# Applying the RMSNorm row factor after the up projection in a two-layer decoder trunk

## The chip, the cores and the metric

The kernel runs on one core of one Trainium2 chip. The metric is the device time of one execution in microseconds. A core has a matrix engine (TensorE, PE in the rows, with its weight loads as PEld), VectorE (DVE), ScalarE (ACT), GpSimd (POOL) and SyncE (SP), and 16 DMA engines. Matmul results land in PSUM banks, all other tiles lie in SBUF.

## What is computed

One inference step of a two-layer decoder trunk for a prompt of 1024 tokens and 8 single-token samples that share the weights. Layer 0 mixes with an RG-LRU, layer 1 with windowed attention; both add attention over a memory. The change lies in the second part of each layer: the output projection, the norm ahead of the feed-forward network, and its up projection, a depthwise convolution of width 3 over tokens, and the gating.

```python
def _rmsnorm(x, g):
    r = lax.rsqrt(jnp.mean(x32 * x32, axis=-1, keepdims=True) + EPS)
    return (x32 * r * g.astype(jnp.float32)).astype(x.dtype)
...
def _conv_ffn(x, buf, w_up, cw, cb, w_down):
    u = x @ w_up
    u, nbuf = _causal_dwconv(u, buf, cw, cb)
    return (jax.nn.gelu(u[..., :D_FF]) * u[..., D_FF:]) @ w_down, nbuf
...
        x = x + jnp.concatenate([main, mo], axis=-1) @ prm['w_out'][l]
        hn = _rmsnorm(x, prm['norm_ffn_g'][l])
        f, fc = _conv_ffn(hn, ffn_conv0[l], prm['w_ffn_up'][l], ...)
        x = x + f
```

The model width is 1024, the network's inner width 3072 (so the up product has 6144 columns), all in float32. The row factor `r` is one number for each token.

## The kernel before

**Layout.** Activations are kept transposed: 128 features on the partitions, 1032 tokens (1024 prompt, 8 sample) along the free axis, so a tensor of 1024 features is eight row tiles (`KD`). Tokens are cut into two halves of 516 (`HALF`) and four quarters of 258 (`QW`). Each float32 product is made of three matmuls in a reduced format: both operands are split into a high part (a ScalarE copy, L105) and a low part (raw minus high, on POOL, L116, or DVE, L113), and `mm3` (L296) issues high×high (L298), high×low (L299), low×high (L300).

**Output projection** (`out_proj`, L775). For each token half and each of eight feature tiles `m`, 24 matmuls for either quarter go to a PSUM bank, and DVE adds the bank to the residual row `x[m]` (L786). `residual` (L769) loads that row when tile `m` begins in the first half, from the input in layer 0 and from a spilled copy in layer 1. `on_tile` (L1322) then stores the quarter to DRAM (`rD`, from SP's queue), squares it on ScalarE and adds it into a running sum. The weight of the next tile is loaded and split one tile ahead: `get` issues a 1024-column copy on ScalarE and a subtraction on POOL.

**Norm and operands.** The up projection is a 2×2 block product in seven products P1 to P7 instead of eight, on blocks B11, B21, B22 and their combinations T1 to T4 (of the row tiles 0–3 and 4–7 and of the two quarters of a half). When a half of `out_proj` is done, `norm(hf)` (L1345) starts: `inverse` (L1332) sums over features by a matmul with ones (L1335) and forms `r` by Ln, Exp and a correction step; then DVE scales each row by gain and `r`, forms the T blocks and splits all seven sets of four operands. It is a generator that is advanced once a tile. So half 0's norm runs beside half 1's tiles and half 1's beside the first products of the up projection; `need` forces what a product still lacks.

**Up projection** (`ffn`, L862). The columns are taken as 24 pairs `j` of a gate tile and a value tile. `ENTRY` gives pair 0's fourteen half-products, then `SEQUENCE` the seven products of each pair over both halves, 24 matmuls a product. `combine` makes each product's weight: sums and differences of four raw blocks on POOL (four 512-column ops for a pair), a copy on ScalarE, a subtraction on POOL, so eleven POOL ops and seven copies a pair, five products ahead (`AHEAD`). The results are added up from PSUM into the gate row `ug` and the value row `uv` by DVE (two evictions of 258 columns for a product, ScalarE for P1 and P2). After P3 the task `post(j)` convolves both rows (one ScalarE pass each, two DVE taps each, and an add of 128x8 for the sample columns), takes the gelu on ScalarE, multiplies on DVE and stores the gated row to `gD` from SP's queue (L888). Each task goes on by one step a product (`tick`). The down projection reads `gD` and `rD` back.

**Order.** ScalarE keeps the written program order in layer 0 up to L1536 and in the second layer's `ffn` (manual schedule, L62). All other engines, and ScalarE elsewhere, get their order from a scheduler that models time. SP issues every transfer of the program before the change.

## Time and profile before

| | us |
|---|---|
| median of three runs | 2533.31 |
| lowest, highest | 2531.02, 2534.02 |
| the profiled execution | 2532.97 |
| its span | 2531.2 |
| layer 0: output projection and pair 0 (335.3 to 521.7) | 186.4 |
| layer 0: up projection of pairs 1 to 23 (521.7 to 990.2) | 468.5 |
| layer 1: output projection and pair 0 (1614.9 to 1783.9) | 169.0 |
| layer 1: up projection of pairs 1 to 23 (1783.9 to 2252.8) | 468.9 |

The page gives each engine's busy time over the whole span. "Windows" cut the span into stretches and give busy time, instructions and the granted TensorE clock (1.00 is the 2.4 GHz level, 0.50 the 1.2 GHz one; a value between is a mixture). "Waits" sum up an engine's idle time by what ended it. "Timeline" lists single instructions or runs of like ones, with the idle time before them and its releaser. "Groups by form" add up all instructions of one line and shape. Matmuls of the two projections have 258 columns.

### The profile page before, as it was taken

The numbers are of one execution on the slowest core, as the hardware profiler recorded it, in microseconds if no ns is written. First come the engines' busy times: TensorE is split into PE (matmuls) and PEld (weight loads), VectorE is DVE, ScalarE is ACT, GpSimd is POOL, SyncE is SP. The second block draws the span as 40 slices with busy tenths as digits, with TensorE's granted clock in tenths as the row PEclk, the third lists the DMA queues.
The fourth block names the chain that finished last, engine by engine and source line by source line (L and its number), as shares of the span: only waits on it lengthen the run. The fifth ranks groups of instructions, "written<-read, shape, count | busy, mean of one in ns | idle before, by whom it ended". The sixth has DMA issues, their size and how long they took to land. (4 is left out here: it accounts for less than half of the span.)

```text
span 2531.2 us, 42857 instructions
## 1 busy us (share of the span) xinstructions
PE 2336.5 (92%) x16590; PEld 2251.5 (89%) x16590; DVE 1549.6 (61%) x2826; ACT 1103.5 (44%) x2277; POOL 1428.0 (56%) x1123
## 2 busy tenths in 40 slices
PE   7997877799999999999989988787999999999999
PEld 5896866799999999999977787677999999999999
DVE  6658955666666666332478789875666566663321
ACT  5567753344433444211365577643443444442110
POOL 2149843588888885322144346435888888853220
PEclk9998989899999999999999999899999999999999
DMA  4221124212222225421575543551222222253311
GB/s 163 87 69 56 58 83 143 63 67 84 84 85 76 76 76 199 150 95 52 178 252 162 185 152 129 163 157 63 77 86 82 76 76 76 76 224 123 101 55 63
DMA packets 142491, 273.64 MB, mean 108 GB/s; under 512 B 28544, under 2 KB 85456, under 8 KB 142288
## 3 DMA queue, kind: packets, MB, share of 16 engines
q1 hardware_dynamic: 142288, 270.91, 31.9%
q8 instruction: 130, 2.13, 0.3%
q14 instruction: 73, 0.60, 0.1%
HBM read 211.99 MB, written 58.87 MB: 107 GB/s over the span
## 5 line engine op out<-in xcount | busy, mean ns | idle before, releaser
L116 POOL TENSOR_TENSOR row<-row,row 128x512 fp32r<-128x512 f32 (+9 forms) x754 | 1153.8, 1552 | 793.9 <-ACT row L105 476.4
L298 PE MATMUL ps<-row,row 128*128 128x258 f32 (+4 forms) x5032 | 1510.4, 303 | 55.5 <-ACT row L105 45.7
L299 PE MATMUL ps<-row,row 128*128 128x258 f32 (+4 forms) x5032 | 1509.1, 302 | 22.5 <-DVE row L113 18.7
L300 PE MATMUL ps<-row,row 128*128 128x258 f32 (+4 forms) x5032 | 1472.7, 301 | 23.5 <-POOL row L116 23.5
L298 PEld LDWEIGHTS ps<-row,row 128*128 128x128 f32 x5032 | 962.3, 191 | 73.9 <-ACT row L105 51.0
L299 PEld LDWEIGHTS ps<-row,row 128*128 128x128 f32 x5032 | 964.0, 192 | 40.2 <-DVE row L113 24.3
L300 PEld LDWEIGHTS ps<-row,row 128*128 128x128 f32 x5032 | 948.4, 192 | 34.1 <-POOL row L116 27.1
L105 ACT ACTIVATE row<-row 128x512 fp32r<-128x512 f32 (+8 forms) x768 | 505.4, 696 | 911.7 <-POOL row L116 305.4
L113 DVE TENSOR_TENSOR row<-row,ps 128x258 f32<-128x258 f32 (+2 forms) x736 | 322.3, 444 | 706.0 <-PE ps L300 666.5
L119 DVE SCALAR_TENSOR_TENSOR row<-row,fw,row 128x1023 f32<-128x1023 f32 x192 | 266.9, 1409 | 67.3 <-ACT row L105 67.3
L113 DVE TENSOR_TENSOR row<-row,row 128x258 fp32r<-128x258 f32 (+8 forms) x262 | 232.9, 912 | 31.3 <-ACT row L105 18.0
L105 ACT ACTIVATE row<-ps 128x258 f32<-128x258 f32 (+6 forms) x430 | 157.5, 406 | 69.6 <-PE ps L300 25.8
L116 POOL TENSOR_TENSOR row<-row,ty 128x768 f32<-128x768 f32 (+2 forms) x56 | 77.2, 1378 | 155.1 <-DVE ty L413 51.3
L105 ACT ACTIVATE row<-row,fw 128x1032 f32<-128x1032 f32 x96 | 114.9, 1245 | 68.8 <-DVE row L113 68.7
L105 ACT ACTIVATE sm<-row 128x258 f32<-128x258 f32 (+3 forms) x130 | 54.5, 452 | 153.5 <-DVE row L113 127.2
L113 DVE TENSOR_TENSOR row<-row,sb 128x8 f32<-128x8 f32 x96 | 102.3, 1066 | 0.0
L113 DVE TENSOR_TENSOR sm<-sm,sm 128x258 f32<-128x258 f32 (+5 forms) x125 | 81.9, 660 | 28.2 <-ACT sm L105 25.7
L105 ACT ACTIVATE row<-ps,ty,ty 128x256 f32<-128x256 f32 (+1 forms) x160 | 87.4, 564 | 10.1 <-DVE ty L113 7.6
L105 ACT ACTIVATE sm<-ps 128x384 f32<-128x384 f32 (+5 forms) x156 | 65.0, 444 | 39.2 <-PE ps L431 21.6
L113 DVE TENSOR_TENSOR row<-ps,row 128x384 fp32r<-128x384 f32 (+2 forms) x125 | 63.5, 519 | 25.1 <-ACT row L105 10.2
L119 DVE SCALAR_TENSOR_TENSOR row<-sm,pack,row 128x384 f32<-128x384 f32 (+1 forms) x54 | 62.6, 1162 | 14.6 <-POOL row L124 13.3
L116 POOL TENSOR_TENSOR sm<-sm,row 128x192 f32<-128x192 f32 (+3 forms) x72 | 49.5, 702 | 36.1 <-ACT sm L105 18.6
(163 smaller groups left out, 1497.3 us busy)
## 6 DMA issues: line engine op xcount, KB each, us to landing
row<-in_w_ffn_up SPq DMA_DIRECT2D x96, 512.0 KB, 3.3
gD<-row SPq DMA_DIRECT2D x48, 516.0 KB, 2.6
row<-gD SPq DMA_DIRECT2D x48, 516.0 KB, 5.6
row<-in_w_ffn_down SPq DMA_DIRECT2D x64, 384.0 KB, 3.1
row<-hD SPq DMA_DIRECT2D x48, 512.0 KB, 6.6
row<-in_w_out SPq DMA_DIRECT2D x32, 512.0 KB, 4.2
rD<-row SPq DMA_DIRECT2D x64, 129.0 KB, 1.9
row<-rD SPq DMA_DIRECT2D x16, 516.0 KB, 8.7
```

What stands on the lines that cost most here:

```text
L105: return nc.scalar.activation(out, in_, func, **kw)
L113: return V.tensor_tensor(out=out, in0=a, in1=b, op=op)
L116: return G.tensor_tensor(out=out, in0=a, in1=b, op=op)
L119: return V.scalar_tensor_tensor(out=out, in0=a, scalar=s, in1=b, op0=op0, op1=op1)
L298: T.matmul(out, ah, bh, start=first and j == 0, stop=False, skip_group_check=more)
L299: T.matmul(out, ah, bl, start=False, stop=False, skip_group_check=more)
L300: T.matmul(out, al, bh, start=False, stop=last and j == n - 1, skip_group_check=more)
```

## The change

The row factor leaves the operands. The gain is applied when a tile of the output projection is finished: DVE adds PSUM and residual into a small tile, ScalarE writes it back scaled by the gain, stores the small tile to `rD` from its own queue and squares it. The blocks T2, T3, T4 are formed and split during `out_proj` from these unscaled rows (`combine_x`, one row pair as soon as its two tiles are there, hence the tile order `TILES`), and B11, B21, B22 and T1 by 516-column splits afterwards (`settle`). `norm` is gone. The inverse root of all four quarters is formed at the eighth half-product (`factor`) into one row, and DVE multiplies that row into each pair's finished `uv` after P4 and into `ug` after P3 (`scale`).

Residual rows are fetched one ahead, by half. `combine` works in place in the raw weight rows (`PREPARED` gives the order), with eleven POOL ops a pair as before, and pair 0's weights are made during the first half of `out_proj` instead of the second. In `post` the value row is convolved first, gelu comes two steps later, and the gated row is stored from ScalarE's queue. The sample columns are taken out of these steps: `samples` finishes them for twelve pairs at once on POOL. The transposes of layer-0 sample memory attention come two steps later, and two output stores move behind `out_proj`.

```diff
+PREPARED = ("P1", "P7", "P6", "P2", "P5", "P4", "P3")
...
+TILES = (0, 4, 1, 5, 2, 6, 3, 7)
...
         yield
+        yield
+        yield
         t = ps()
         for k in range(2):
...
-    def residual(l, m):
+    def residual(l, hb, kk):
+        t = row()
         if l:
-            return unspill(m)
-        t = row()
-        SY.dma_start(t[:, :NT], I["x_t"][:, m, :])
+            unspill(t, hb, kk)
+        else:
+            SY.dma_start(
+                t[:, : 2 * HALF].rearrange("p (a t) -> p a t", a=2),
+                I["x_t"].rearrange("p (a k) t -> p a k t", a=2)[:, :, kk, hb * HALF : hb * HALF + HALF],
+            )
         return t
...
     def out_proj(l, mget, ks, x, on_tile, on_half):
+        ahead = deque((hb, kk) for hb in range(2) for kk in range(4))
+
+        def fetch():
+            if ahead:
+                hb, kk = ahead.popleft()
+                x[hb, kk] = residual(l, hb, kk)
+
+        fetch()
         for hb in range(2):
-            for m in range(KD):
+            for m in TILES:
                 key = f"out{l}.{hb}.{m}"
                 wh, wl = get(key, 1, 1)
-                if x[m] is None:
-                    x[m] = residual(l, m)
-                for q in (2 * hb, 2 * hb + 1):
-                    c0 = QB[q]
+                if m < 4:
+                    fetch()
+                for part in range(2):
+                    c0 = QB[2 * hb + part]
                     p = ps()
                     mm3(p[:, :QW], [(wh[:, k * P : k * P + P], wl[:, k * P : k * P + P]) + mget(k, c0, QW) for k in ks])
-                    vtt(x[m][:, c0 : c0 + QW], x[m][:, c0 : c0 + QW], p[:, :QW], add)
-                    on_tile(q, m)
+                    on_tile(hb, part, m, p[:, :QW])
                     tick()
                 drop(key)
...
-                src = R["G"][:, lo_]
+                src = G[:, lo_]
+            elif name == "P7":
+                src = G[:, lo_]
+                gtt(src, src, V_[:, lo_], sub)
             elif name == "P6":
-                S = R["S"] = row()
-                gtt(S[:, lo_], R["V"][:, lo_], R["V"][:, hi_], add)
-                gtt(S[:, hi_], S[:, lo_], R["G"][:, lo_], sub)
-                src = S[:, hi_]
+                src = G[:, lo_]
+                gtt(src, V_[:, hi_], src, sub)
             elif name == "P2":
-                src = R["G"][:, hi_]
-            elif name == "P7":
-                src = R["G"][:, lo_]
-                gtt(src, src, R["V"][:, lo_], sub)
+                src = G[:, hi_]
             elif name == "P5":
-                src = R["S"][:, lo_]
+                src = V_[:, lo_]
+                gtt(src, src, V_[:, hi_], add)
             elif name == "P4":
-                src = R["V"][:, hi_]
+                src = V_[:, hi_]
             else:
-                src = R["S"][:, hi_]
-                gtt(src, R["G"][:, hi_], src, sub)
+                src = G[:, hi_]
+                gtt(src, src, G[:, lo_], sub)
             w = row(F32R)
             acopy(w[:, lo_], src)
             gtt(w[:, hi_], src, f(w[:, lo_]), sub)
...
+        def scale(u):
+            vtt(u[:, :NT], u[:, :NT], factor()[:, :NT], mul)
...
-            vtt(a[:, SEQ:NT], a[:, SEQ:NT], sb3[:, :, t], add)
...
         def post(j):
             ug, uv = st.pop(j)
+            scale(ug)
+            av = act_conv(uv, KF + j)
+            yield
+            taps(av, uv, KF + j)
+            del uv
             ag = act_conv(ug, j)
             yield
             taps(ag, ug, j)
             del ug
-            av = act_conv(uv, KF + j)
-            yield
-            taps(av, uv, KF + j)
-            del uv
-            act(ag[:, :NT], ag[:, :NT], AF.Gelu_apprx_tanh)
-            yield
-            vtt(ag[:, :NT], ag[:, :NT], av[:, :NT], mul)
-            SY.dma_start(gD[l, j], ag[:, :NT])
-            yield
+            yield
+            act(ag[:, :SEQ], ag[:, :SEQ], AF.Gelu_apprx_tanh)
+            yield
+            vtt(ag[:, :SEQ], ag[:, :SEQ], av[:, :SEQ], mul)
+            if j % SG == SG - 1:
+                samples(j - SG + 1)
+            yield
+            nc.scalar.dma_start(gD[l, j, :, :SEQ], ag[:, :SEQ])
+
...
+            if name == "P4" and hfs[-1] == 1:
+                scale(st[j][1])
             if name == "P3" and hfs[-1] == 1:
                 return start(post(j))
...
-        todo = [(0, p) for p in STEADY] + [(j, p) for j, p, _ in SEQUENCE if j]
+        todo = [(j, p) for j in range(KF) for p in PREPARED]
         at = 7
         for q, (j, name, hfs) in enumerate(SEQUENCE):
-            if q == 6:
+            if q == 2:
                 load_pair(1)
-            want = 7 if q < 10 else min(len(todo), q - 7 + AHEAD)
+            if q == 8:
+                factor()
+            want = 7 + max(0, q - 4) // 2 if q < 14 else min(len(todo), q - 7 + AHEAD)
...
-        def on_tile(q, m):
-            SY.dma_start(rD[l, m, :, cols(q)], x[m][:, cols(q)])
...
+        def on_tile(hf, part, m, p):
+            q = 2 * hf + part
+            xs, t = place(hf, part, m), sm()
+            vtt(t[:, :QW], xs, p, add)
+            acopy(xs, t[:, :QW], scale=g_ffn[l][m])
+            nc.scalar.dma_start(rD[l, m, :, QB[q] : QB[q] + QW], t[:, :QW])
...
+                s = sm()
+                act(s[:, :QW], t[:, :QW], AF.Square)
+                vtt(sums[q][:, :QW], sums[q][:, :QW], s[:, :QW], add)
+            if part == 0 and wait:
+                combine_x(*wait.pop())
+            if part == 1 and m >= 4:
+                wait.append((hf, m - 4))
+
+        def combine_x(hf, kk):
+            a, b = place(hf, 0, kk), place(hf, 1, kk)
+            c, d = place(hf, 0, kk + 4), place(hf, 1, kk + 4)
+            t3, t2, t4 = (sm()[:, :QW] for _ in range(3))
+            vtt(t3, d, b, sub)
+            vtt(b, b, a, sub)
+            vtt(t2, d, b, sub)
+            vtt(t4, c, t2, sub)
+            for name, t in (("T3", t3), ("T2", t2), ("T4", t4)):
+                if kk % 2 == 0:
+                    own[name] = row(F32R)
+                o = (kk % 2) * HALF
+                split(name, kk, hf, own[name][:, o : o + QW], own[name][:, o + QW : o + HALF], t)
...
+        def settle(hf):
+            cs = slice(hf * HALF, hf * HALF + HALF)
+            for kk in range(4):
+                for a, names in enumerate((("B11", "T1"), ("B21", "B22"))):
+                    k = kk + 4 * a
+                    hi, lo, raw = mh[k][:, cs], ml[k][:, cs], x[hf, kk][:, a * HALF : a * HALF + HALF]
+                    acopy(hi, raw)
+                    (gtt if a else vtt)(lo, raw, f(hi), sub)
+                    for part, name in enumerate(names):
+                        o = slice(hf * HALF + part * QW, hf * HALF + part * QW + QW)
+                        ops[name, kk, hf] = mh[k][:, o], ml[k][:, o]
+                del x[hf, kk]
+                yield
...
         def inverse(q):
+            if not rf:
+                rf.append(row())
             a = sums.pop(q)
             p = ps()
...
+            m, t, r = sm()[:, :QW], sm()[:, :QW], a[:, :QW]
             ts(V, m, p[:, :QW], 1.0 / D, EPS, mul, add)
-            act(out, m, AF.Ln)
...
-        def norm(hf):
-            qa, qb = cols(2 * hf), cols(2 * hf + 1)
-            ra, rb = inverse(2 * hf), inverse(2 * hf + 1)
...
+            act(r, m, AF.Ln)
+            act(r, r, AF.Exp, scale=-0.5)
+            stt(t, m, -0.5, r, mul, mul)
+            vtt(t, t, r, mul)
+            stt(rf[0][:, QB[q] : QB[q] + QW], t, 1.5, r, add, mul)
...
-            for name in STEADY:
+            for name in PREPARED:
                 weights[1](0, name)
                 yield
...
+        gen["w"] = spawn(first_pair())
...
         def on_half(hf):
+            if wait:
+                combine_x(*wait.pop())
             if hf:
                 finish(gen["w"])
-            gen[hf] = start(norm(hf))
-            if not hf:
-                gen["w"] = spawn(first_pair())
+            gen[hf] = start(settle(hf))
...
+        def factor():
+            for q in sorted(sums):
+                inverse(q)
+            return rf[0]
```

ScalarE in the second half of layer 0's output projection, a tile and the next weight's split (the last row), before: `sm` rows are squares, 1024 columns a weight, the 258-column copies `norm`'s operands.

```order
L105 ACTIVATE sm_4219<-row_3601 128x258
L105 ACTIVATE row_3484<-row_3805 128x258
L105 ACTIVATE row_4229<-row_3805 128x258
L105 ACTIVATE row_3488<-row_3873 128x258
L105 ACTIVATE row_4229<-row_3873 128x258
L105 ACTIVATE sm_4268<-row_3601 128x258
L105 ACTIVATE row_3460<-row_3941 128x258
L105 ACTIVATE row_4278<-row_3941 128x258
L105 ACTIVATE row_3464<-row_4009 128x258
L105 ACTIVATE row_4278<-row_4009 128x258
L105 ACTIVATE row_4290<-row_4141 128x512
L105 ACTIVATE row_4293<-row_4190 128x1024
```

And after: `sm`, `pack` to `row` is the scaled row written back, `rD` a store, three copies from `sm` the T blocks.

```order
L108 ACTIVATE row_4339<-row_4269 128x1024
L108 ACTIVATE row_4193<-sm_4372,pack 128x258
L1374 DMA rD<-sm_4372 128x258
L108 ACTIVATE sm_4376<-sm_4372 128x258
L108 ACTIVATE row_4386<-sm_4379 128x258
L108 ACTIVATE row_4389<-sm_4380 128x258
L108 ACTIVATE row_4392<-sm_4381 128x258
L108 ACTIVATE row_4193<-sm_4420,pack 128x258
L1374 DMA rD<-sm_4420 128x258
L108 ACTIVATE sm_4424<-sm_4420 128x258
L108 ACTIVATE row_4427<-row_4343 128x1024
```

The operand copies of `norm` are gone; between two weight splits stand two write-backs, two stores, two squares and, in this tile, three operand copies.

DVE in one pair of the up projection, before: 258-column rows are evictions from `ps`, the taps are on line L119, `row_7419` and `row_7425` are the two convolved rows.

```order
L119 SCALAR_TENSOR_TENSOR row_7419<-row_7258,fw,row_7419 128x1023
L113 TENSOR_TENSOR row_7419<-row_7419,sb 128x8
L119 SCALAR_TENSOR_TENSOR row_7425<-row_7222,fw,row_7425 128x1023
L113 TENSOR_TENSOR row_7425<-row_7425,sb 128x8
L119 SCALAR_TENSOR_TENSOR row_7419<-row_7258,fw,row_7419 128x1022
L119 SCALAR_TENSOR_TENSOR row_7425<-row_7222,fw,row_7425 128x1022
L113 TENSOR_TENSOR row_7493<-row_7457,ps_7467 128x258
L113 TENSOR_TENSOR row_7493<-row_7457,ps_7480 128x258
L113 TENSOR_TENSOR row_7419<-row_7419,row_7425 128x1032
```

And after: `row_4954` is the row of factors, `row_7468` the value row, `row_7502` the gate row; the taps are on line L122.

```order
L116 TENSOR_TENSOR row_7468<-row_7468,row_4954 128x1032
L116 TENSOR_TENSOR row_7502<-row_7502,ps_7575 128x258
L116 TENSOR_TENSOR row_7502<-row_7502,ps_7588 128x258
L116 TENSOR_TENSOR row_7502<-row_7502,row_4954 128x1032
L122 SCALAR_TENSOR_TENSOR row_7664<-row_7468,fw,row_7664 128x1023
L122 SCALAR_TENSOR_TENSOR row_7664<-row_7468,fw,row_7664 128x1022
L122 SCALAR_TENSOR_TENSOR row_7669<-row_7502,fw,row_7669 128x1023
L116 TENSOR_TENSOR row_7736<-row_7702,ps_7710 128x258
L116 TENSOR_TENSOR row_7736<-row_7702,ps_7723 128x258
L122 SCALAR_TENSOR_TENSOR row_7669<-row_7502,fw,row_7669 128x1022
L116 TENSOR_TENSOR row_7669<-row_7669,row_7664 128x1024
```

Two products of 1032 columns have come in and the two 8-column adds have gone. The second product and three taps stand ahead of the next pair's evictions.

## Rows read from the trace of the kernel before

**Rows 1.** Page, part 1: busy time, share of the span, instructions of each engine.

```profile
PE 2336.5 (92%) x16590; PEld 2251.5 (89%) x16590; DVE 1549.6 (61%) x2826; ACT 1103.5 (44%) x2277; POOL 1428.0 (56%) x1123
```

**Rows 2.** Windows, layer 0: stretch, us, busy time (instructions) by engine, clock, DMA share, GB/s.

```profile
335.30:352.00 16.70, 7.98 (x28) 6.50 (x29) 11.99 (x21) 5.75 (x13) 5.91 (x4) 0.50 0.16 41
335.30:405.50 70.20, 53.82 (x384) 51.07 (x384) 29.40 (x53) 21.70 (x45) 28.43 (x17) 0.86 0.41 125
405.50:413.10 7.60, 1.81 (x8) 1.32 (x6) 1.80 (x5) 2.05 (x3) 1.70 (x1) 0.80 0.57 181
413.10:485.00 71.90, 55.30 (x387) 53.79 (x386) 48.72 (x82) 26.79 (x61) 43.31 (x32) 0.83 0.27 86
485.00:521.70 36.70, 27.39 (x172) 23.80 (x171) 29.00 (x65) 14.76 (x40) 15.79 (x19) 0.86 0.19 62
```

**Rows 3.** Windows, layer 1: the same columns.

```profile
1614.90:1674.10 59.20, 54.61 (x424) 52.69 (x421) 40.54 (x86) 26.57 (x55) 25.54 (x15) 0.97 0.88 258
1674.10:1680.90 6.80, 2.54 (x7) 1.43 (x7) 4.08 (x11) 2.09 (x5) 0.06 (x1) 0.67 0.27 97
1680.90:1746.60 65.70, 51.58 (x387) 50.62 (x385) 41.37 (x81) 25.72 (x57) 40.52 (x30) 0.88 0.19 63
1746.60:1783.90 37.30, 27.90 (x173) 24.29 (x172) 28.93 (x65) 14.83 (x40) 15.82 (x19) 0.86 0.18 61
```

**Rows 4.** Waits of TensorE, 335.3 to 521.7: waited for, total us, times, longest.

```profile
PE ps L298 <- ACT row L105: 26.7, 10, 8.2
PE ps L300 <- POOL row L116: 12.4, 9, 2.0
PE ps L1335 <- DVE sm L113: 6.8, 2, 5.8
```

**Rows 5.** Timeline, one tile of half 0: start us, us, instruction, count [idle before].

```profile
366.21 0.76 DVE L113 TENSOR_TENSOR row<-row,ps 128x258 f32<-128x258 f32 x2 [5.96 <-DMA row<-in_x_t]
...
366.67 0.80 SPq L1323 DMA_DIRECT2D rD<-row  x2
368.01 0.45 SPq L772 DMA_DIRECT2D row<-in_x_t  x1
...
367.33 1.04 ACT L105 ACTIVATE row<-row 128x1024 fp32r<-128x1024 f32 x1
...
368.45 2.39 POOL L116 TENSOR_TENSOR row<-row,row 128x1024 fp32r<-128x1024 f32 x1 [4.37 <-ACT row L105]
```

**Rows 6.** Timeline, ScalarE in the second half of layer 1.

```profile
1702.33 2.56 ACT L105 ACTIVATE row<-row 128x258 fp32r<-128x258 f32 x5 [0.93 <-DVE row L113]
```

**Rows 7.** Windows, layer 0: the up projection of pairs 1 to 23.

```profile
521.70:990.20 468.50, 466.15 (x3866) 465.56 (x3865) 300.36 (x395) 198.07 (x326) 393.19 (x297) 1.00 0.24 83
```

**Rows 8.** Groups by form, 600 to 900: count | busy us, mean ns | idle before, releaser.

```profile
L116 POOL TENSOR_TENSOR row<-row,row 128x512 fp32r<-128x512 f32 x105 | 165.3, 1592 | 44.8 <-ACT row L105 44.8
L113 DVE TENSOR_TENSOR row<-row,row 128x1032 f32<-128x1032 f32 x15 | 18.3, 1222 | 0.0
L105 ACT ACTIVATE row<-row 128x1032 f32<-128x1032 f32 x15 | 16.0, 1069 | 64.6 <-DVE row L119 64.6
```

**Rows 9.** Timeline, POOL and then DVE in a steady pair.

```profile
699.51 2.53 POOL L116 TENSOR_TENSOR row<-row,row 128x512 fp32r<-128x512 f32 x2
701.98 0.20 POOL L867 COPY ul<-row 128x10 f32<-128x10 f32 x1
709.52 2.29 POOL L116 TENSOR_TENSOR row<-row,row 128x512 fp32r<-128x512 f32 x1
...
708.19 1.26 DVE L113 TENSOR_TENSOR row<-row,sb 128x8 f32<-128x8 f32 x1
711.76 2.47 DVE L119 SCALAR_TENSOR_TENSOR row<-row,fw,row 128x1022 f32<-128x1022 f32 x2
```

**Rows 10.** Waits of TensorE, 200 to 335.

```profile
PE ps L729 <- DVE sm L123: 12.6, 1, 12.6
```

**Rows 11.** Waits of TensorE, 975 to 1010, end of the up projection.

```profile
PE ps L298 <- DVE row L113: 2.0, 1, 2.0
```

More of the change, by code (lines that the diff above doesn't have):

```diff
@@ L37 @@
 DCH = 6
+SG = 12
 NDC = KF // DCH
@@ L851, in combine, with ffn @@
             made[j, name] = w
-            R["n"] = R.get("n", 0) + 1
-            if R["n"] == 7:
+            if name == "P3":
                 raws[j] = None
         return load_pair, combine, made
-    def ffn(l, x, ops, need, weights, on_block, store=None):
+    def ffn(l, ops, need, factor, weights, on_block, store=None):
         ul3 = ul.rearrange("p (c t) -> p c t", c=10)
@@ L1512, in r_of @@
         return rcol[:np_, i : i + 1], rsq[:np_, i : i + 1]
-    ffn(0, x, ops, need, uw, handB)
+    ffn(0, ops, need, rowf, uw, handB)
     x = None
```

129 lines of the change are left out of this document (51 added, 78 removed).

## The prediction

> **What bounds the kernel now.** I read the utilisation page first, then busy time by stretch, then TensorE's waits inside the stretches with gaps, then single instructions. TensorE (PE) is busy 92% of the span [rows 1], but not evenly. The up projection of each layer (23 of its 24 column pairs) runs gap-free at granted clock 1.00, the 2.4 GHz level: 3866 matmuls in 468.5 us in layer 0, 0.1212 us each [rows 7]. The gaps are ahead of it, in the output projection and pair 0 (the "entry"): 335.3 to 521.7, 186.4 us, in layer 0 [rows 2], and 1614.9 to 1783.9, 169.0 us, in layer 1 [rows 3]. Each holds 936 matmuls of that size, 113.5 us at 0.1212; so 73 us of layer 0's stretch and 55.5 of layer 1's are not full-speed matmul time. PE's waits there name three things [rows 4]: ScalarE's weight split (26.7 us, longest 8.2), POOL's part of it (12.4 in nine) and the inverse root (6.8). The granted clocks of 0.83 to 0.86 say that a stall costs a second time: part of what follows runs at the 1.2 GHz level.
>
> In the up projection PE hides everything else, but only just. A DVE instruction with two SBUF inputs and a POOL instruction do not overlap here: two POOL ops alone take 2.53 us, 1.27 each; the one that meets a DVE tap takes 2.29, and a tap alone 1.23 (two in 2.47) [rows 9]. A meeting pair thus takes about 2.25 us instead of 2.50. Per pair, alone, before: 11 POOL ops (13.75), four taps and a product (6.0), and four pieces of 8 or 10 columns (0.6, by the 0.20 of POOL's 10-column copy), 20.4 us; a pair lasts 468.5/23 = 20.37. That is the place where this change can lose.
>
> **Part by part.** My sum is against the profiled execution's own 2532.97 us (span 2531.2), 0.3 below the median of 2533.31 and inside the runs shown.
>
> *Residual rows fetched ahead, row stores on ScalarE's queue, half 0.* Now SP issues the next residual row behind two row stores (0.80 us) and a weight load; DVE sits 5.96 us idle for it, and POOL's split waits 4.37 behind ScalarE, which waits for that DVE add [rows 5]. Six such stalls of 1.1 to 1.7 us fall in half 0 of layer 0, some 8 us. They go. Against that, pair 0's combining (11 POOL ops, 13.8 us) moves from half 1 into half 0, with operand combining on top: per row pair seven DVE ops of about 0.4 us and three copies of 0.51 [rows 6]. ScalarE is in program order here, so two store issues (0.40 us each, the price SP pays) now stand ahead of each weight split. I take 4 us of the 8 as kept. The first 16.7 us of the stretch wait for the mixer's last rows and don't change. Half 0: 70.2 to 66, −4. In layer 1 half 0 is nearly clean (59.2 us for 424 matmuls), so only the added load remains: +5.
>
> *The inverse leaves the half boundary.* The 7.6 us there (6.8 in layer 1) [rows 2, 3] are mostly PE standing at the column-sum matmul. After, nothing but the next weight split stands there: eviction 0.38, copy 0.51, issue 0.40, square 0.51, split copy 1.04 and POOL's 2.39 [rows 5, 6], some 5.2 us after the last tile, minus what a weight split one tile ahead covers. I take 4: −3.6 and −2.8.
>
> *No normalisation of half 0 during half 1.* Now 28 operand splits and 16 row-factor products run there, and ScalarE's weight split stands behind runs of five 258-column copies (2.56 us) [rows 6]. After, half 1 has what half 0 has plus eight 516-wide copies of settle(). 384 matmuls plus two entry-size gaps: I take 48.5 us (46.5 at 0.1212, plus 2), −23.4 from 71.9 and −17.2 from 65.7 [rows 2, 3].
>
> *The entry.* Now PE waits for half 1's operands, one by one: 36.7 and 37.3 us for 172 matmuls, 20.8 at 0.1212. After, T2, T3 and T4 are ready, the first seven half-products use half 0's operands (10 us of cover), and settle(1) needs eight copies of about 0.6, by the 1.04 of a 1024-column one (5 us). The factor for four quarters comes at the eighth half-product, and PE does not wait for it. I take 25 us, since the clock starts low: −11.7 and −12.3.
>
> Stages together: −42.7 in layer 0 and −27.3 in layer 1, −70.
>
> *The row factor in the up projection.* Each pair gains two 128x1032 products (1.22 us each, as the existing product is) [rows 8] and loses two 8-column adds. Those adds show 1.26 us each but that is waiting for POOL [rows 9]; their own work is no more than the 0.20 of a 10-column copy. POOL keeps 11 ops. Alone, a pair now needs 13.75 + 7 × 1.2 + 0.3 = 22.45 us on the shared path, and each DVE op that meets a POOL op takes 0.22 off: 20.9 if all seven meet, against PE's 20.37. ScalarE's gelu now waits 64.6 us in 15 pairs for DVE's taps, and POOL 44.8 behind ScalarE [rows 8]; in that 3 us hole two taps run without a meeting. The gelu is issued two ticks later after the change, which closes the hole; I take five of seven as meeting: 21.35 us. That is 0.98 above PE, and with a buffer of five prepared weights in front the first pair or two don't feel it: 22 × 0.98 × 2 layers = +43 us. Bounds: 20.37 (+0) and 22.45 (+92).
>
> The Trainium skill, page "SBUF — State Buffer", section "Who interferes with whom", says that a VectorE instruction with two SBUF inputs takes a port pair shared with GpSimd as an exclusive lock, so that one blocks the other for its whole length. It speaks against this change; the trace agrees but for the 0.2 us that a meeting saves, and strictly by it the price would be the +92 end.
>
> *Gated-row stores from ScalarE's queue:* one issue per pair, about 0.4 us on an engine that is busy 198 of 468.5 us [rows 7], after its data were ready: 0; if DVE's product were late it would hold a weight split, and that is in R1. *Combining in place:* same 11 POOL ops, a row less: 0. *Two ticks later transposes of the sample memory rows:* PE stands 12.6 us there for DVE's last product before them [rows 10]; other matmuls can go ahead only if they are ready, and they come from the same DVE queue: −1 (0 to −12). *Tail:* the last pair's stall of 2.0 us [rows 11] grows a little since scale, convolution, gelu come later: +3 for both layers (0 to +5).
>
> Sum: −70 − 1 + 43 + 3 = −25: **2508 us**.
>
> **Rivals.** *R1, the shared path decides (slower).* If DVE's products arrive when POOL has nothing queued, because POOL again waits for ScalarE and ScalarE for DVE, few meet and a pair needs about 22.45 us. For: P7 now follows P6 at once, so DVE's eviction of P6 stands behind a row product and up to three taps in the same in-order queue (the DVE order shown with the change); one late eviction holds a PSUM bank and PE. Against: the gelu wait that makes POOL's hole is moved. Price +92 and, with some of the stage gains lost to the same load (53 left), 2533 + 92 + 3 − 53 = **2575**. It decides from about 21.9 us a pair, where 44 × 1.55 us eats the 70 gained. *R2, the path does not bind.* The 20.4 us need was met in 20.37 with POOL waiting 3 us a pair; with that hole filled, and the 8-column adds' waiting gone, 20.37 stays: 2533 − 70 − 1 + 3 = **2465**. *R3, half 1 gives its gain back.* The weight splits stay behind ScalarE's in-order work (copies, store issues, squares, three operand copies per row pair), so that half 1 and the boundary gain half: 35 instead of 70, with 43 lost: 2533 − 35 − 1 + 43 + 3 = **2543**.
>
> **How the numbers follow.** Forecast 0.56 (own range 2480 to 2532: 20.9 to 21.7 us a pair, 60 to 75 gained), R1 0.18, R2 0.14, R3 0.12. The range 2465 to 2552 takes in R2 and R3 and leaves out R1. About 0.2%, 5 us, is what a measurement here can tell from no change. Faster by more: 0.50 of the forecast, R2's 0.14 and little else, 0.65; within: 0.07; slower: R1 0.18 and most of R3, some of the forecast's upper end, 0.28.
>
> **What would show it.** Right: out-projection stretches without DVE idle on residual rows, no wait at the column-sum matmul between halves, half 1 near 48 us, the entry near 25, a steady pair near 21.3 us with PE waiting for POOL's weight parts and POOL near 100% with DVE. R1: a pair of 22 us or more, with waits of PE for DVE evictions beside POOL. R2: 20.4 a pair. R3: half 1 above 55 us with waits for ScalarE's split. Wrong altogether: a steady clock below 1.00, so that PE pays twice for gaps inside the up projection (a pair with two 1 us gaps at the lower level would cost more than the gaps), or a scheduler order on DVE in which row products hold evictions all through.

## The result and the profile after

The changed kernel takes 2558.43 us (median of four runs), the kernel before 2532.86 beside it: a ratio of 1.010, interval 1.0083 to 1.0118. It is slower by 25 us where 25 us faster was forecast, and the time lies above the range. The profiled execution has a span of 2555.5 us against 2531.2. One of e3's four runs below took 4932.79 us, nearly twice the others, and is left out of e3's time.

First the stretches of [rows 2], [rows 3] and [rows 7] in the changed kernel: us, busy time and instructions of PE, PEld, DVE, ACT, POOL, granted clock, DMA share, GB/s. In either kernel the two projections of a layer are 4800 matmuls of 258 columns, and the bounds lie behind the same number of them: 384, 768, 936 and 4800.

```profile
335.40:403.50 68.10, 56.15 (x386) 53.79 (x386) 53.16 (x80) 34.57 (x75) 42.48 (x27) 0.85 0.39 129
403.50:454.10 50.60, 48.24 (x386) 47.76 (x386) 33.74 (x63) 28.50 (x59) 23.09 (x12) 0.97 0.39 125
454.10:477.30 23.20, 22.13 (x179) 21.70 (x178) 16.60 (x37) 13.15 (x28) 10.29 (x8) 1.00 0.23 79
477.30:979.40 502.10, 476.92 (x3867) 467.50 (x3866) 373.39 (x397) 195.91 (x328) 456.46 (x302) 1.00 0.22 77
1619.30:1686.60 67.30, 56.47 (x423) 53.79 (x421) 47.97 (x104) 36.20 (x80) 35.06 (x20) 0.92 0.65 190
1686.60:1699.30 12.70, 0.04 (x2) 0.01 (x1) 12.53 (x15) 6.67 (x15) 10.36 (x10) 0.64 0.52 156
1699.30:1748.40 49.10, 48.47 (x385) 48.26 (x386) 31.50 (x59) 23.93 (x54) 14.51 (x6) 0.95 0.37 116
1748.40:1770.20 21.80, 21.80 (x178) 21.58 (x177) 17.89 (x36) 11.17 (x26) 11.81 (x9) 1.00 0.24 80
1770.20:2270.60 500.40, 476.48 (x3866) 467.21 (x3865) 370.77 (x396) 195.87 (x327) 455.34 (x301) 1.00 0.22 77
```

| stretch | before | forecast | after | after − before |
|---|---|---|---|---|
| layer 0: first half | 70.2 | 66 | 68.1 | −2.1 |
| layer 0: half boundary | 7.6 | 4 | 0 | −7.6 |
| layer 0: second half | 71.9 | 48.5 | 50.6 | −21.3 |
| layer 0: entry (pair 0) | 36.7 | 25 | 23.2 | −13.5 |
| layer 0: pairs 1 to 23 | 468.5 | 490 | 502.1 | +33.6 |
| down projection and layer 1's mixer | 624.7 | 626 | 639.9 | +15.2 |
| layer 1: first half | 59.2 | 64 | 67.3 | +8.1 |
| layer 1: half boundary | 6.8 | 4 | 12.7 | +5.9 |
| layer 1: second half | 65.7 | 48.5 | 49.1 | −16.6 |
| layer 1: entry | 37.3 | 25 | 21.8 | −15.5 |
| layer 1: pairs 1 to 23 | 468.9 | 490 | 500.4 | +31.5 |
| down projection of layer 1 | 278.4 | 280 | 284.9 | +6.5 |

The long stretches without a row of their own are the differences between the bounds of their neighbours. In layer 0 the output projection and the entry gained what was forecast (44.5 us against 42.7); layer 1 gained 18.1 instead of 27.3. The up projection lost 65 us instead of 43, and some 22 us went into what follows it, where 3 were forecast.

The up projection is no longer gap-free. ScalarE's evictions of P1 (the first of two in each pair, start in us first) give the pair's length: 21.52 us at its steadiest (769.66 to 791.18), and 23.96 and 22.36 around 740, where `samples` has its turn.

```profile
723.34 0.63 ACT L108 ACTIVATE row<-ps 128x258 f32<-128x258 f32 x2
...
747.30 0.63 ACT L108 ACTIVATE row<-ps 128x258 f32<-128x258 f32 x2
...
769.66 0.63 ACT L108 ACTIVATE row<-ps 128x258 f32<-128x258 f32 x2
...
791.18 0.63 ACT L108 ACTIVATE row<-ps 128x258 f32<-128x258 f32 x2
```

In 770 to 920 the kernel before has 1251 matmuls, 20.14 us for the 168 of a pair (windows, same columns):

```profile
770.00:920.00 150.00, 150.00 (x1251) 150.00 (x1250) 95.84 (x129) 62.07 (x104) 126.13 (x96) 1.00 0.24 85
```

The changed one has 1173, which is 21.48 us, and PE waits once a pair for POOL's part of a weight (waits: us, times, longest):

```profile
770.00:920.00 150.00, 144.19 (x1173) 141.61 (x1172) 110.30 (x120) 57.32 (x98) 138.49 (x91) 1.00 0.21 75
```

```profile
PE ps L303 <- POOL row L119: 5.8, 7, 0.9
```

By form (count | busy, mean ns | idle before), the weight parts on POOL have gone from 1592 ns [rows 8] to 1826, and a product by the row factor takes 1843 ns, where a product of that size took 1222 [rows 8]. The difference is time in which one of the two engines waits for the other, as e5 below bears out.

```profile
L119 POOL TENSOR_TENSOR row<-row,row 128x512 fp32r<-128x512 f32 x49 | 88.9, 1826 | 9.4 <-ACT row L108 9.4
L122 DVE SCALAR_TENSOR_TENSOR row<-row,fw,row 128x1022 f32<-128x1022 f32 x14 | 26.9, 1923 | 0.2
L116 DVE TENSOR_TENSOR row<-row,row 128x1032 f32<-128x1032 f32 x14 | 25.8, 1843 | 1.3 <-DVE row L116 0.5
```

### The profile page after: what moved, and what is told of

The parts are those of the page before. It is cut to its first block, busy times and chain, and to the rows that moved or that the text cites. A ratio compares the mean times of both kernels' runs of the same rounds, so it can differ in the third digit from the quotient of the medians.

```text
span 2555.5 us, 42979 instructions
## 1 busy us (share of the span) xinstructions
PE 2344.0 (92%) x16590; PEld 2250.7 (88%) x16590; DVE 1703.8 (67%) x2772; ACT 1120.4 (44%) x2313; POOL 1541.3 (60%) x1103
## 4 chain that ended last, share of the span: by engine, by line
PE 32%; POOL 30%; issue 13%; DVE 11%; ACT 5%; DMA 1%; SPq 0%; POOLq 0%; ACTq 0%; DVEq 0%
POOL row L119 27%; PE ps L303 10%; PE ps L301 10%; PE ps L302 10%; ACT row L108 4%; DVE row L116 3%; POOL ul L894 2%; DVE row L122 2%; DVE sm L116 2%; DVE ty L116 1%; ACT sm L108 1%; POOL sm L119 1%; DVE ty L399 1%; DVE row L1209 1%; DVE ty L122 0%
## 5 line engine op out<-in xcount | busy, mean ns | idle before, releaser
L119 POOL TENSOR_TENSOR row<-row,row 128x512 fp32r<-128x512 f32 (+9 forms) x666 | 1105.7, 1671 | 688.6 <-ACT row L108 381.5
L108 ACT ACTIVATE row<-row 128x512 fp32r<-128x512 f32 (+9 forms) x688 | 487.3, 738 | 980.5 <-POOL row L119 369.8
L116 DVE TENSOR_TENSOR row<-row,ps 128x258 f32<-128x258 f32 (+2 forms) x672 | 287.2, 444 | 467.7 <-PE ps L303 464.8
L116 DVE TENSOR_TENSOR row<-row,row 128x1032 f32<-128x1032 f32 (+8 forms) x286 | 388.8, 1371 | 110.9 <-ACT row L108 95.3
L122 DVE SCALAR_TENSOR_TENSOR row<-row,fw,row 128x1023 f32<-128x1023 f32 x192 | 349.8, 1841 | 60.9 <-POOL ul L894 47.8
L119 POOL TENSOR_TENSOR row<-row,ty 128x768 f32<-128x768 f32 (+2 forms) x56 | 77.1, 1377 | 165.7 <-DVE ty L416 62.6
L119 POOL TENSOR_TENSOR row<-row 128x512 f32<-128x512 f32 x96 | 163.3, 1701 | 6.7
L108 ACT ACTIVATE row<-row,fw 128x1024 f32<-128x1024 f32 x96 | 114.2, 1230 | 13.1 <-DVE row L116 13.1
L116 DVE TENSOR_TENSOR sm<-sm,sm 128x258 f32<-128x258 f32 (+5 forms) x125 | 90.2, 724 | 32.1 <-ACT sm L108 29.2
L894 POOL COPY ul<-row 128x10 f32<-128x10 f32 x96 | 67.8, 706 | 9.2 <-DVE row L116 9.2
L119 POOL TENSOR_TENSOR sm<-sm,row 128x192 f32<-128x192 f32 (+3 forms) x72 | 48.9, 694 | 37.8 <-DVE sm L116 18.3
L122 DVE SCALAR_TENSOR_TENSOR row<-sm,pack,row 128x384 f32<-128x384 f32 (+1 forms) x54 | 59.1, 1097 | 14.0 <-POOL row L127 13.4
```

The costliest lines, as they stand in the source:

```text
L108: return nc.scalar.activation(out, in_, func, **kw)
L116: return V.tensor_tensor(out=out, in0=a, in1=b, op=op)
L119: return G.tensor_tensor(out=out, in0=a, in1=b, op=op)
L122: return V.scalar_tensor_tensor(out=out, in0=a, scalar=s, in1=b, op0=op0, op1=op1)
L894: G.tensor_copy(out=ul3[:, :, t], in_=u[:, SEQ - 2 : NT])
```

## Experiments

Ratios are against the kernel before, measured beside each group. "Pair" is 150 us × 168 divided by the matmuls in 770 to 920, a stretch behind `samples`' first turn.

**e1: no factor products.**

```diff
         def scale(u):
-            vtt(u[:, :NT], u[:, :NT], factor()[:, :NT], mul)
+            pass
```

> The changed kernel without the two products by the row factor in the up projection (the factor is still formed, the rows stay unscaled, so the result is not the norm's). Theory A, these two products by themselves fill the path that DVE and POOL share: a steady pair falls from 21.52 to about 20.2 us, 44 pairs x 1.3 = 58 us, so about 2500 us. Theory B, the new order (weights made as P1, P7, P6, value row first, gelu later, stores on ScalarE's queue) is what slows the pair: it stays above 21 us, so above 2535 us.

2490.96 us, ratio 0.9835 (0.982 to 0.9849). The pair is 20.19 us and PE does not stop (windows, 770 to 920):

```profile
770.00:920.00 150.00, 150.00 (x1248) 149.88 (x1247) 93.51 (x113) 63.81 (x108) 138.38 (x97) 1.00 0.22 76
```

So all other parts of the change, the new weight order, the order of `post` and the stores on ScalarE's queue, cost nothing in a steady pair. Theory B falls as far as these parts alone are meant.

**e3: the kernel before, plus two products.**

```diff
+        one = row()
+        V.memset(one[:, :NT], 1.0)
...
+            if name == "P4" and hfs[-1] == 1:
+                vtt(st[j][1][:, :NT], st[j][1][:, :NT], one[:, :NT], mul)
...
             ug, uv = st.pop(j)
+            vtt(ug[:, :NT], ug[:, :NT], one[:, :NT], mul)
```

> The kernel before with two 1032-column products by a row of ones in each pair, at the places where the change has them (value row after P4, gate row at the start of the post step); nothing else of the change. Theory A: the pair rises from 20.2 to 21.5 us or, as the old order fills POOL's hole less well, to 22.4; 2533 + 58 to 97, 2590 to 2630 us. Theory B: little, the 20.2 us pair stays under 20.6, below 2550 us.

2624.33 us, ratio 1.0367 (1.035 to 1.0385). The pair is 21.99 us:

```profile
770.00:920.00 150.00, 142.18 (x1146) 138.40 (x1146) 113.20 (x132) 55.42 (x93) 129.59 (x89) 1.00 0.20 75
```

Two products of 1032 columns, added alone, slow the old kernel by 93 us. They are dearer here (21.99) than in the changed kernel (21.48). That fits the closing of POOL's hole: POOL stands 19.9 us behind ScalarE in e3, and 9.4 us in the changed kernel (same stretch; its row stands in the section before). It is not shown apart, as no run changes the order of `post` alone.

```profile
L116 POOL TENSOR_TENSOR row<-row,row 128x512 fp32r<-128x512 f32 x47 | 80.6, 1731 | 19.9 <-ACT row L105 19.9
```

**e2: the factors in PSUM.**

```diff
         def scale(u):
-            vtt(u[:, :NT], u[:, :NT], factor()[:, :NT], mul)
+            for h in range(2):
+                cs = slice(512 * h, 512 * h + 512)
+                vtt(u[:, cs], u[:, cs], bank["rf", h], mul)
...
-            G.tensor_copy(out=ul3[:, :, t], in_=u[:, SEQ - 2 : NT])
+            acopy(ul3[:, 0:2, t], u[:, SEQ - 2 : SEQ])
+            gtt(ul3[:, 2:10, t], u[:, SEQ:NT], factor()[:, SEQ:NT], mul)
...
                 factor()
+                for h in range(2):
+                    bank["rf", h] = ps()
+                    acopy(bank["rf", h], factor()[:, 512 * h : 512 * h + 512])
...
+        factor(True)
+        bank.clear()
...
```

> The changed kernel with the factors of the 1024 prompt tokens held in two PSUM banks: the same products, the same place in DVE's order, but one operand from PSUM, each in two pieces of 512 columns; the eight sample columns are scaled by POOL where it copied them. Theory A (both operands from SBUF are what counts): a pair of 20.2 to 20.5 us, 2500 to 2515 us. Theory B (DVE's time, its queue, or the waits for the product): a pair of 21.4 us or more, 2555 us or more; with six banks left instead of eight PE may also wait for a bank, which would show as waits of PE for evictions.

2594.69 us, ratio 1.025 (1.0235 to 1.0266): slower, as theory B had it and not theory A. The windows row shows why this is no verdict on theory A: POOL is busy 113 us instead of 138, so the shared path is not full, and the clock is 0.95.

```profile
770.00:920.00 150.00, 139.77 (x1108) 138.96 (x1106) 99.01 (x126) 56.13 (x104) 113.26 (x87) 0.95 0.19 66
```

In every second pair the scheduler put the second half of the gate row's product behind both taps of the value row (DVE, timeline):

```profile
641.62 1.94 DVE L122 SCALAR_TENSOR_TENSOR row<-row,fw,row 128x1023 f32<-128x1023 f32 x1 [1.96 <-ACT ul L108]
643.49 0.41 DVE L116 TENSOR_TENSOR row<-row,ps 128x258 f32<-128x258 f32 x1
643.82 1.98 DVE L122 SCALAR_TENSOR_TENSOR row<-row,fw,row 128x1022 f32<-128x1022 f32 x1
645.72 0.68 DVE L116 TENSOR_TENSOR row<-row,ps 128x512 f32<-128x512 f32 x1
```

ScalarE, in program order, stood before the gate row's convolution until 646.48 (the trace names no releaser; DVE's second half ends at 646.40), and the next weight split (647.72) behind it; PE waited 2.75 us for that split. In 770 to 920, with three such stops, the granted clock was 0.95 (row above).

```profile
646.48 1.24 ACT L108 ACTIVATE row<-row,fw 128x1024 f32<-128x1024 f32 x1 [4.87 <-issue]
...
647.72 0.61 ACT L108 ACTIVATE row<-row 128x512 fp32r<-128x512 f32 x1
```

```profile
648.39 0.51 PE L301 MATMUL ps<-row,row 128*128 128x258 f32 x1 [2.75 <-ACT row L108]
```

A wait that the edit itself had made hid its effect. e5 removes the wait, and e9 is its counter-check.

**e5: e2, with the gate row's convolution one step later.**

```diff
             taps(av, uv, KF + j)
             del uv
+            yield
             ag = act_conv(ug, j)
```

> e2 with one step more between the value row's taps and the gate row's convolution. In e2 pairs alternated between 19.4 and 25.6 us: in every second pair DVE's second half of the gate row's product stood behind the value row's taps, ScalarE waited for it in program order and the next weight split behind that, while DVE and POOL together were busy only 87% of the time. Theory A: with that wait gone the pair is 20.2 to 20.6 us and the run about 2500 us. Theory B (factor products cost DVE's queue or PSUM banks, whatever the operand): pair above 21.3 us, above 2550 us.

2502.48 us, ratio 0.989 (0.9874 to 0.9906), faster than both kernels. The pair is 20.16 us without a gap:

```profile
770.00:920.00 150.00, 150.00 (x1250) 150.00 (x1249) 114.42 (x140) 65.57 (x123) 139.57 (x98) 1.00 0.22 75
```

**e9: that step alone, factors in SBUF.** The diff is e5's, on the changed kernel.

> The changed kernel with the one step more between the value row's taps and the gate row's convolution that e5 has, but with the factors in SBUF. Theory A (two SBUF operands): the pair stays at 21.2 us or more and the run at 2545 us or more. If the step alone made e5's gain, the pair is 20.2 to 20.5 us and the run near 2500 us.

2587.79 us, ratio 1.0223 (1.0208 to 1.0238); pair 22.24 us:

```profile
770.00:920.00 150.00, 141.25 (x1133) 136.90 (x1132) 105.88 (x114) 58.93 (x97) 139.16 (x89) 1.00 0.21 71
```

The step by itself makes it worse. So e5's gain over e9, 85 us and 2.08 us a pair, goes with the one operand that was moved from SBUF to PSUM, with the halving and the sample columns' own steps that this needed; the products and their place in the program are the same. Halving alone, with the factors in SBUF, was not run. What speaks against it as the cause: an add of only 8 columns with two SBUF operands still took 1.26 us while POOL worked [rows 9], so a short piece does not escape the wait. In e5 the two halves of a product take 684 ns each, with POOL busy for 139.57 of 150 us, so 1.37 us for the product; the taps, which still have two SBUF operands, stay long (by form):

```profile
L122 DVE SCALAR_TENSOR_TENSOR row<-row,fw,row 128x1022 f32<-128x1022 f32 x16 | 30.9, 1928 | 0.0
L116 DVE TENSOR_TENSOR row<-row,ps 128x512 f32<-128x512 f32 x29 | 19.8, 684 | 0.7
```

**e10: one product instead of two.**

```diff
             ug, uv = st.pop(j)
-            scale(ug)
```

> The changed kernel with the gate row left unscaled (so the result is not the norm's); the value row's product stays. Theory A with additive use of the shared path: 21.52 less one product of 1.2 us is 20.3, so a pair of 20.2 to 20.5 us and about 2500 us. If the place of the two products in DVE's order mattered more than their sum, the pair would stay above 20.9 us, 2530 us or more.

2528.88 us, ratio 0.9989 (0.998 to 0.9999); pair 21.07 us, not 20.3. The cost is not additive: leaving out the second product gives back 0.4 us of 1.3. What remains is a wait of 0.7 us in each pair for DVE:

```profile
PE ps L301 <- DVE row L116: 4.8, 7, 0.7
```

DVE runs the four taps in one piece of 6.57 us (four alone would take 4.9, by the two of [rows 9]); the next pair's P6 evictions stand behind them, and PE behind those. So the sum of the work on the shared path is not all that counts: sharing it also made this burst on DVE longer than the slack of one eviction.

```profile
669.68 6.57 DVE L122 SCALAR_TENSOR_TENSOR row<-row,fw,row 128x1023 f32<-128x1023 f32 x4 [2.03 <-ACT row L108]
676.17 0.74 DVE L116 TENSOR_TENSOR row<-row,ps 128x258 f32<-128x258 f32 x2
```

**e6: layer 1's last mixer rows loaded early.**

```diff
                 if m < 4:
                     fetch()
+                if l and hb == 0 and m == 2:
+                    start_m(2)
```

> The changed kernel with the loading of the last token block of layer 1's mixer rows started during the first half of the output projection, not at the second half's first tile. Theory D (these eight loads stand on SP's queue behind the pieces of the second half's residual rows, which in turn wait for tiles still to be stored): the 12.65 us gap at layer 1's half boundary falls under 4 us; 2546 to 2550 us. Theory C2 (no free row buffer for them, whatever the order): the gap stays or moves, 2555 to 2562 us.

2545.52 us, ratio 1.0066 (1.0048 to 1.0084), 13 us less than the changed kernel. In the two traces 8.5 us of it lie between layer 1's first matmul of the output projection and the last P2 eviction of its up projection; the rest lies in stretches where e6 changes nothing. In the changed kernel PE stood 12.7 us at layer 1's half boundary, the longest of these three waits:

```profile
PE ps L301 <- ACT row L108: 22.7, 3, 12.7
```

for splits of mixer rows whose loads SP issued only at 1690.86, behind the pieces of the second half's residual rows:

```profile
1686.47 0.32 SPq L564 DMA_DIRECT2D row<-xD  x1
1686.83 0.43 SPq L565 DMA_DIRECT2D row<-xD  x1
1687.31 0.48 SPq L568 DMA_DIRECT2D row<-xD  x1
1690.86 4.72 SPq L1860 DMA_DIRECT2D row<-mD  x8
```

SP itself had waited for row stores to finish, which now sit on ScalarE's queue (SP's waits, 1640 to 1700):

```profile
SPq L565 <- DMA rD<-sm: 7.1, 1, 7.1
SPq L1860 <- DMA rD<-sm: 3.0, 1, 3.0
```

The trace also shows how a load comes to wait for a store of another queue. The 791 transfers of the program signal eight semaphores, 98 or 99 each, and a load such as those on L565 waits for the one that it signals itself. The wait of 7.1 us ends with the load at 1675.48, which has the same semaphore as a row store that ScalarE issued only at 1673.48.

With the loads started in the first half, SP issues them from 1657.69 (timeline) and PE passes the boundary at 1685.6 without a stop; what is left is the wait of 7.9 us at the second tile and one of 2.2 us at 1673.05, still in the first half.

```profile
1657.69 4.82 SPq L1862 DMA_DIRECT2D row<-mD  x4
...
1663.11 2.88 SPq L1862 DMA_DIRECT2D row<-mD  x4
```

```profile
PE ps L301 <- ACT row L108: 10.1, 2, 7.9
PE ps L303 <- POOL row L119: 3.4, 4, 1.3
```

**e4: pair 0 later in layer 1.**

```diff
-        gen["w"] = spawn(first_pair())
+        if l == 0:
+            gen["w"] = spawn(first_pair())
...
             gen[hf] = start(settle(hf))
+            if l and not hf:
+                gen["w"] = spawn(first_pair())
```

> The changed kernel, but in layer 1 pair 0's weights are made during the second half of the output projection, as before the change. Theory C, row buffers: the nine rows that pair 0 holds in the first half keep the mixer rows of the last token block from being loaded, so PE stands 12.65 us at the half boundary; then that gap falls under 4 us and the run to about 2548 us (part is given back in half 1). Theory D, the pieces of spilled residual rows and the order on SP's queue: the gap stays over 9 us, about 2558 us.

2550.34 us, ratio 1.0073 (1.0056 to 1.009). The boundary's wait stays at 11.9 us, so theory C, row buffers held by pair 0, falls. The three waits together fall from 22.7 to 17.2 us, nearly all of it at the second tile (8.6 to 3.8), which I had not told apart from the boundary.

```profile
PE ps L301 <- ACT row L108: 17.2, 3, 11.9
```

**e7: the row of factors given back.** `factor(True)` clears it after the last pair.

> The changed kernel with the row of factors given back after the last pair; in the change its buffer stays taken through the down projection and layer 1's mixer. If that one buffer is why the stretch from the down projection's end to layer 1's output projection is some 8 us longer than before, it is back within 2 us: about 2550 us. If the scheduler's other order there is the cause, 2556 to 2561 us or any other value within 10 us, with the mixer's gaps at other places.

2558.71 us, ratio 1.0114 (1.0098 to 1.013): no change. The buffer is not the cause.

**e8: stores back on SP's queue.** Both `nc.scalar.dma_start` of the change become `SY.dma_start`.

> The changed kernel with the row stores and the gated-row stores issued from SP's queue, as before the change. If store issues on ScalarE's queue held up weight splits, the pair falls below 21.4 us and the out projection gets shorter, 2550 us or less. If they cost nothing there, 2555 to 2562 us; if SP then holds the prefetched rows behind stores, the out projections get longer, 2565 us or more.

2556.45 us, ratio 1.0105 (1.0087 to 1.0123): no difference that can be measured. The pair stays at 21.5 us, and the longest wait in layer 1's output projection at 12.2 us; the queue of the stores was worth nothing either way.

**e11 and e12: together.** e11 is e5 with e6, e12 is e11 with e4.

> e5 and e6 together: factors in PSUM, the later convolution, the mixer's last rows loaded early. e5 gave 2502 us, e6 took 13 us off the changed kernel at a place that e5 leaves as it was: 2488 us, 2484 to 2498 with the 5 to 10 us by which the mixer's stretch differs between kernels.

> e11 with pair 0's weights of layer 1 made in the second half, as in e4. In e4 the first wait of layer 1's output projection fell from 8.55 to 3.8 us and its second half took over little: 4 us less than e11, so about 2484 us; if the second half has no room for the eleven POOL operations now that its gap is gone, equal or up to 4 us more.

e11: 2494.39 us, ratio 0.9855 (0.9838 to 0.9872), at the slow end of its expectation. e12: 2487.13 us, ratio 0.9825 (0.981 to 0.984), 7 us less than e11 and, with e15 below, the best here: 45 us faster than the kernel before, 71 faster than the changed one. By the traces 4.6 of the 7 us lie in layer 1's mixer (359.5 and 354.9 us), which e12's edit does not touch, so its own share is nearer 3 than 7.

**e13, e14, e15: the two further steps ahead of the transposes.** The change's text ahead of the prediction puts them in layer 0's mixer; the routine is called in both layers. e13 takes them out of the changed kernel, e14 puts them into the kernel before, e15 takes them out of e12.

```diff
         ts(V, pt[:32, :256], pt[:32, :256], rd[:32, :1], None, mul, None)
         yield
-        yield
-        yield
         t = ps()
```

> The changed kernel without the two further steps ahead of the transposes in the sample rows' memory attention, which both layers' mixers call. Theory E, these steps lengthen layer 1's mixer: from the last eviction of the down projection to the first matmul of the output projection it is back at 348 to 350 us from 356, and the run near 2551 us, provided layer 0's mixer stays as it is (its 12.6 us stop at the transposes may come back, with nothing gained or lost over 1 us at 335 us). Theory F, the scheduler's new order of that stretch whatever the edit: it stays anywhere from 351 to 365 us.

> The kernel before with those two steps alone. Theory E: layer 1's mixer goes from 348 to about 356 us, 2540 us. Theory F: any value from 346 to 360, and nothing else changes; the output projection of layer 0 begins within 1 us of 335.3 in either case, as what the transposes waited for is DVE's work.

> e12 without the two steps. Theory E: e12's 354.9 us of layer 1's mixer becomes about 348 and the run about 2480 us. Theory F: 2480 to 2497 us with the mixer anywhere from 350 to 362.

e13: 2555.71 us, ratio 1.0089 (1.0074 to 1.0104), with 355.1 us in the stretch in question; e14: 2541.72 us, 1.0035 (1.0023 to 1.0048), with 358.9; e15: 2489.1 us, 0.9828 (0.9813 to 0.9843), with 352.4. Taking the steps out gives nothing back beyond 3 us, so theory E falls as the cause in the changed kernel. e14 comes out as theory E said for the mixer (347.9 to 358.9) but lies among the 351 to 365 us of kernels with other edits, so it does not tell the steps from any other edit; and its output projection of layer 0 begins at 331.7 us, not within 1 us of 335.3.

## Why the prediction was wrong, step by step

In the forecast's terms: the stages gained 62.6 us instead of 70, the up projection lost 65 instead of 43, and what follows the up projection lost 22 where 3 were forecast.

- **Output projection and entry, layer 0: right.** Half 1 at 50.6 us (48.5 forecast), the entry at 23.2 (25), the boundary without a stop. R3 did not happen.
- **The same in layer 1: the mechanism right, one wait missed.** Second half and entry came out as forecast or better (49.1 and 21.8). The step that failed is the +5 for half 0 and the 4 us for the boundary, which came out as +8.1 and 12.7. I took layer 0's boundary for both, and looked only at ScalarE and POOL; in layer 1 the mixer rows come from DRAM over SP's queue, and the change puts the residual rows of the second half, in smaller pieces, ahead of the last of them. That queue should have been followed row by row. e6 took the gap at the boundary away.
- **The up projection: the term was mis-sized, 43 for 65.** The mechanism is shown by e1 (none: 20.19 us), e3 (two products alone on the old kernel: 21.99), and e5 against e9 (20.16 and 22.24: the operand's place, with the halving and the sample steps that it needed). Three parts of the size failed. The base: I called the stretch gap-free and took 468.5/23 = 20.37 as PE's own pair, but a steady pair before is 20.14. The stretch also holds slower work at its end, with the 2.0 us stop of [rows 11] and a lower clock:

```profile
970.00:990.20 20.20, 18.20 (x139) 18.03 (x139) 16.20 (x20) 8.34 (x13) 10.39 (x7) 0.92 0.56 197
```

  The need: 21.35 forecast, 21.48 measured. By the forecast's own reckoning that is between four and five meetings in seven; no run counts them. Base and need together make 1.34 us a pair instead of 0.98, over 23 pairs a layer and not 22: 62 us. And `samples`, which I did not cost: two pairs of 23.96 and 22.36, 3.3 us a layer over 21.52. These make 68 us, of which some 3 come back, as the first and last pairs stand out less from the steady ones than before. That `samples` is what lengthens the two pairs is read from its place and size, not from a run without it. Its five small POOL operations take 3.8 us of POOL, four of them 0.8 us apiece where the fifth takes 0.4 (POOL, timeline):

```profile
726.52 1.65 POOL L119 TENSOR_TENSOR sm<-ul,fw 128x96 f32<-128x96 f32 x2
...
729.39 1.71 POOL L119 TENSOR_TENSOR sm<-sm,sb 128x96 f32<-128x96 f32 x2
...
734.55 0.40 POOL L119 TENSOR_TENSOR sm<-sm,sm 128x96 f32<-128x96 f32 x1
```

- **The order on DVE.** R1 named the late P6 eviction as its mechanism. In the change itself PE waits for POOL (5.8 us in seven pairs); the late eviction is what e9 and e10 show. R1's price came from the sum of all work alone (22.45), and e9's 22.24 is near that end. R2, a path that does not bind, falls with the 65 us. Of the four pair lengths with products from SBUF (21.07 in e10, 21.48 in the change, 21.99 in e3, 22.24 in e9) the forecast's 21.35 comes near the change's own only, so that nearness is partly luck.
- **The tail and what follows: +22 instead of +3.** By the bounds above 13 us are the ends of the two up projections and the down projections behind them. A part of it is where the stop falls: before, it stood ahead of pair 23's last matmuls and counted with the pairs, now it stands behind them. The last pair's gelu now comes two steps later, ScalarE stands 5.43 us for its taps in program order, and the first down weight's split (994.00) behind it; PE waits 3.6 us for it, after 2.7 us in two waits for DVE's splits.

```profile
PE ps L301 <- ACT row L108: 3.6, 1, 3.6
```

```profile
991.28 1.06 ACT L108 ACTIVATE row<-row 128x1024 f32<-128x1024 f32 x1 [5.43 <-DVE row L122]
...
994.00 0.84 ACT L108 ACTIVATE row<-row 128x768 fp32r<-128x768 f32 x1 [1.49 <-DVE row L116]
```

- **The transposes in layer 0's mixer: −1 forecast, 0 measured.** PE's 12.6 us stop at L729 [rows 10] is gone from the changed kernel and is spread over eight waits for ScalarE (waits, 200 to 335). The output projection begins at 335.4 us instead of 335.3, and at 333.0 in e13, where the stop is back. In the other kernels with the two steps that leave this part alone it begins at 331.8 to 335.1 us, so a single us cannot be told here.

```profile
PE ps L301 <- ACT sm L108: 15.1, 8, 4.6
```

- **Layer 1's mixer: open.** From the last eviction of the down projection to the first matmul of the output projection it takes 356.2 us instead of 347.9. e3, whose edits touch only the up projection, has 353.7, and the other kernels here 351 to 365; the kernel before is the shortest of all. The factor's row buffer (e7) and the two steps (e13) are not the cause. A new order from the scheduler with each edit is not the whole of it either: in this stretch PE runs the same sequence of matmuls, by line and shape, in e7 as in the changed kernel, and in e4 but for one place, yet the three differ by 12 us and in granted clock (the changed kernel, e7, e4):

```profile
1263.10:1619.30 356.20, 302.31 (x1848) 263.96 (x1846) 297.91 (x855) 223.82 (x712) 168.37 (x175) 0.95 0.50 164
1263.00:1615.90 352.90, 298.57 (x1848) 258.91 (x1847) 297.34 (x855) 223.84 (x712) 168.66 (x175) 0.97 0.50 166
1260.50:1625.30 364.80, 311.26 (x1846) 269.20 (x1846) 299.61 (x859) 223.98 (x711) 168.50 (x175) 0.93 0.50 161
```

  Each of these lengths is read from one execution, and e4's is the slowest of its four runs (2556.08 us, the others 2547.88 to 2551.86). So the cause of the 8.3 us stays open, and so does how much of it belongs to these single executions alone.

A rule of the Trainium skill, page "SBUF — State Buffer", section "Who interferes with whom", says that a VectorE instruction with at most one SBUF input, outside the two-port modes, does not contend with GpSimd, while one with two contends with a GpSimd instruction that reads SBUF. The trace agrees: 684 ns for half a product with one operand in PSUM, and e5 without a gap on PE. I had cited only its second half, as a price, and not read the first half as the way out.

## What to carry to other kernels

Before work is moved onto DVE, add up by the stretch what DVE instructions with two SBUF operands and POOL need together; a busy share of 61% for DVE said nothing here, while the two together already filled the pair. If they fill it, put an operand that many instructions share into PSUM. Here that took two of the kernel's eight banks and, together with the later convolution, gave back 1.3 us a pair. Measure an alternative with its own new waits in view: e2 would have refuted the right cause.

## What the runs showed of the hardware

- The price of a DVE product beside POOL depends on its neighbours: one product less gave 0.4 us a pair, both 1.3, and one step of delay for a ScalarE pass added 0.75 (e10, e1, e9).
- With a stop of PE of up to 2.9 us in every second pair the mean granted clock was 0.95, a mixture of the 2.4 and 1.2 GHz levels (e2, 770 to 920); with stops of up to 0.9 us in each pair it stayed at 1.00 (the changed kernel, same stretch).
- A store issued from ScalarE's queue held up loads on SP's queue: by the trace's releasers, SP waited up to 7.1 us for a row store to complete before its next transfer. That the stores' own queue is not the point is e8's result: with the stores back on SP's queue the longest wait of PE there is still 12.2 us, of 12.7.
